# A hybrid decoder layer on one core: GpSimd leaves the attention stage, the compressed branch and the scores are spaced anew, the probabilities' factor is shared by VectorE and ScalarE

## The chip, the cores and the metric

One core of a Trainium2 chip runs the whole layer. The metric is the device time in microseconds (us) of one execution; three executions of the kernel before are known, and one more was recorded by the hardware profiler.

## The reference

One layer, 512 positions, width 1024, float32. A normalised input is projected; three mixers (a gated MLP, "a"; sparse attention, "b"; a recurrent block, "c") each go through a matrix of their own, are weighted by a sigmoid gate and summed; then an output projection and a SwiGLU block follow. The change touches the attention and the sum of branch a:

```python
s_c = where(valid_c, qh @ kc.T * scale, NEG_INF)         # compressed: 31 block keys a head
o_cmp = (softmax(s_c) * any(valid_c)) @ vc
o_slc = softmax(masked(q @ k_slc.T * scale)) @ v_slc     # 8 blocks in 512 positions, all of them chosen
o_win = softmax(masked(q @ k_win.T * scale)) @ v_win     # window 512: also plain causal attention
o = g[..., 0:1] * o_cmp + g[..., 1:2] * o_slc + g[..., 2:3] * o_win
merged = gate_a * (y_a @ w_br_a) + gate_b * (y_b @ w_br_b) + gate_c * (y_c @ w_br_c)
```

There are 16 heads in 4 groups; a group shares keys and values. Top 16 of only 8 blocks chooses all, so the selected and the window branch (br 0 and 1) are both causal attention with their own keys and values.

## The kernel before, in words

**Weights.** Every product runs as three passes over a high and a low part of the operands. A weight tile of 128x1024 is fetched by a DMA of the SP queue into one of two `raw` buffers (`wload`, L168), ScalarE copies it to `hi` (L114), and another engine subtracts to get `lo`: VectorE (L119), or GpSimd (L117) for every third tile of the list `wpool`, that is of the weights used in the attention stage (L158, L193). Three `hi` and three `lo` buffers run ahead of TensorE.

**The attention stage** is `attention(fills)` (L868). For each group `g` there is a list of fill work: gates and products of branch a (`gate_part`, `branch_part`), then the two query tiles, the key tile and, for every second group, the value tiles of the next group. A fill generator yields after every 6 matmuls of 512 columns; each yield is a slot. In each slot `steps(g, 22)` gives out a share of the group's attention, planned so that it lasts 22 slots: `scores(j)` of a unit (a block of 128 queries, one or both branches), `turn` (four transposes of probabilities, L838, and their split into `ph` and `pl`), `values` (two matmuls, L851). A turn comes at least 3 slots after its unit's last score (LAG_T), values 3 slots after their turn (LAG_V); at most three turns run ahead of their values; a unit's scores wait until the unit two before it is turned, because `P` has two buffers. Before the key tile of the next group all scores are given out without fill between them (`while kind == "k"`), because the keys have one buffer. What is left of a group when the fill ends follows without fill.

**The compressed branch** of the next group, `cmp_attn(g + 1)` (L749), has seven steps (scores and mask; maximum, difference, exp; sum and product L773; transposes L777; two value products). Before, its generator begins after both query tiles, one step in every third slot while the group's own steps last, and what is left follows in one go at the group's end.

**A unit's tail** (L826 to L833): after the fourth score, VectorE takes the reciprocals of the sums, multiplies by the gates (L829), and multiplies the probabilities by that factor with one TENSOR_SCALAR for each head and branch, 8 for a unit of both branches (128 or 256 wide), 4 for a unit of one branch (384 or 512 wide).

**The sum of branch a** (`branch_part`, L955): VectorE makes the gated product from PSUM (L966), GpSimd adds it to `merged` (L968). Branch b adds on VectorE (L972).

The issue order on each engine is fixed when the program is built: the framework's scheduler sorts instructions by the order in which they were emitted and by when it estimates them ready, so matmuls of later fills can stand ahead of emitted attention work. On the chip each engine takes its list in order.

Of the kernel before, what the change touches and what calls it, by code (L numbers as in the profile page):

```python
# [25 lines left out]
AF = mybir.ActivationFunctionType  # L26
OP = mybir.AluOpType
# [5 lines left out]
G = 4  # L33
# [17 lines left out]
def hybrid_block(ctx: ExitStack, tc: tile.TileContext, A, out):  # L51
    nc = tc.nc
    V, SC, GP, PE, SY = nc.vector, nc.scalar, nc.gpsimd, nc.tensor, nc.sync
# [33 lines left out]
    def nm(s):  # L87
        cnt[0] += 1
        return f"{s}_{cnt[0]}"
# [8 lines left out]
    def bank(tag):  # L98
        return psum[1].tile([128, S], F32, tag=tag, name=nm(tag), bufs=psum[2][tag])
# [10 lines left out]
    def f32(ap):  # L110
        return ap.bitcast(F32)
# [12 lines left out]
    wlist = []  # L124
# [4 lines left out]
    def w_branch(i, j0=0, j1=8):  # L129
        for j in range(j0, j1):  # L130
            w_in(T_MG + 8 * i + j)
            wlist.append((A["w_br"][i, j], None))
# [11 lines left out]
    w_in(*range(T_U, T_U + 8), *range(T_QKV, T_QKV + 3))  # L144
    wlist += [(A["w_vp"][0, i], None) for i in range(2)]
    FILL = (3, 2, 3, 8)
    w0 = len(wlist)
    fill = []
    for j in range(8):
        fill += [(A["w_in"][T_MG + j], None), (A["w_br"][0, j], None)]  # L150
    for g in range(G):
# [3 lines left out]
            w_in(*range(T_QKV + 3 * g + 3, T_QKV + 3 * g + 6))  # L155
        if g == 1:
            wlist += [(A["w_vp"][1, i], None) for i in range(2)]
    wpool = range(w0, len(wlist))  # L158
    w_branch(1)
    wlist += [(A["w_o"][k], t) for k, t in enumerate(["h"] * 4 + ["f"] + ["m"] * 2 + [None])]  # L160
    HEAD, LAST, LASTV = 3, 4, 2
# [6 lines left out]
    def wload(upto):  # L168
        while wnext[0] < min(upto, len(wlist)):
            i = wnext[0]  # L170
            ap, tag = wlist[i]
            raw = stage.tile([128, 1024], F32, tag="raw", name=nm("raw"), bufs=2)
            parts = [slice(0, 512), slice(512, 1024)] if i == 0 else [slice(0, 1024)]
            for n, p in enumerate(parts):
                SY.dma_start(raw[:, p], ap[:, p])
                if i == 0:
                    x_in(n + 1)
            if tag == "gate":

                hi = lo = wts.tile([128, 1024], F32R, tag="hi", name=nm("hi"), bufs=3)  # L180
                SC.activation(hi, raw, AF.Copy)
                r, h = (t.rearrange("p (k m) -> p k m", m=128)[:, :, 64:] for t in (raw, hi))
                V.tensor_sub(h, r, f32(h))
                wready[i] = (hi, lo)
                wnext[0] += 1
                continue
            if tag:
                u = slab("u", F32R, tag, (2, 1024))
                hi, lo = u[:, 0], u[:, 1]
            else:  # L190
                hi = wts.tile([128, 1024], F32R, tag="hi", name=nm("hi"), bufs=3)
                lo = wts.tile([128, 1024], F32R, tag="lo", name=nm("lo"), bufs=3)
            todo = [(raw[:, p], hi[:, p], lo[:, p], GP if i in wpool and i % 3 == 2 else V) for p in parts]  # L193
            if i == 0:
                wfirst.extend(todo)
            else:
                split(*todo[0])
            wready[i] = (hi, lo)
            wnext[0] += 1
# [33 lines left out]
    def x_in(k):  # L233
        SY.dma_start(xt[k], A["xT"][:, k, :])
# [558 lines left out]
    class Unit:  # L793
# [14 lines left out]
        def scores(self, j):  # L808
            g, a, n, brs = self.g, self.a, self.n, self.brs
            w = len(brs)  # L810
            if j == 0:
                self.T = slab("P", tag="P")
                self.st = mid.tile([128, 3, 4, w], F32, tag="ast", name=nm("ast"), bufs=3)
            st, K = self.st, at[g]["k"]
            ps = bank("sc")
            lhs = at[g]["q"][:, j, a * 128:(a + 1) * 128]
            for i in range(2):
                PE.matmul(ps[:, :w * n].rearrange("p (b n) -> p b n", b=w), lhs, K[:, i, brs[0]:brs[-1] + 1, :n],  # L818
                          start=(i == 0), stop=(i == 1))
            for b, br in enumerate(brs):  # L820
                t = self.part(j, br)
                V.tensor_tensor_reduce(out=t, in0=ps[:, b * n:b * n + n], in1=mask[0][:, S - n:], scale=-0.125,  # L822
                                       scalar=3.0e38, op0=OP.add, op1=OP.min, accum_out=st[:, 0, j, b:b + 1])
                SC.activation(t, t, AF.Exp, scale=-1.0, bias=st[:, 0, j, b:b + 1],  # L824
                              accum_out=st[:, 1, j, b:b + 1])
            if j == 3:  # L826
                V.reciprocal(st[:, 2], st[:, 1])
                for b, br in enumerate(brs):
                    V.tensor_mul(st[:, 2, :, b], st[:, 2, :, b], gates[:, a, 12 * g + 1 + br:12 * g + 12:3])  # L829
                for i in range(4):  # L830
                    for b, br in enumerate(brs):
                        t = self.part(i, br)
                        V.tensor_scalar(t, t, st[:, 2, i, b:b + 1], None, op0=OP.mult)  # L833

        def turn(self, br, kt):
            pt = bank("tr")
# [31 lines left out]
    def attention(fills):  # L868


        slot = [0]
        LAG_T, LAG_V, LAG_C = 3, 3, 3

        def steps(g, slots):

            units = [Unit(g, 0, (0, 1)), Unit(g, 1, (0, 1))] + [Unit(g, a, (br,)) for a in range(2, 4) for br in range(2)]
            SQ = [(n, j) for n in range(len(units)) for j in range(4)]
            TQ = [(n, b) for n, u in enumerate(units) for b in u.blocks]
            VQ = list(TQ)
            sdone, tdone, tslot = {}, {}, {}  # L880
            cs = lambda n: 2 * max(107, 53 * (units[n].a + 1)) / 1e3
            left = sum(cs(n) for n, _ in SQ) + len(TQ) * 0.41 + len(VQ) * 0.43
            k = 0
            while SQ or TQ or VQ:
                room = left / max(slots - k, 1)
                k += 1
                t = slot[0]
                ns = 0
                while room > 0:
                    if VQ and tslot.get(VQ[0], 1e9) + LAG_V <= t:  # L890
                        n, b = VQ.pop(0)
                        units[n].values(*b)
                        c = 0.43
                    elif TQ and sdone.get(TQ[0][0], 1e9) + LAG_T <= t and len(TQ) + 3 > len(VQ):
                        n, b = TQ.pop(0)
                        units[n].turn(*b)
                        tslot[n, b] = t
                        if b == units[n].blocks[-1]:
                            tdone[n] = t
                        c = 0.41  # L900
                    elif SQ and ns < 2 and (SQ[0][0] < 2 or SQ[0][0] - 2 in tdone):
                        n, j = SQ.pop(0)
                        ns += 1
                        units[n].scores(j)
                        if j == 3:
                            sdone[n] = t
                        c = cs(n)
                    else:
                        break
                    room -= c  # L910
                    left -= c
                yield bool(SQ)

        for g, fill in enumerate(fills):
            body = steps(g, 22)
            nxt = cmp_attn(g + 1) if g < G - 1 else iter(())
            wait = 0
            more = True
            have_q = 0
            for kind, gen in fill:  # L920
                while kind == "k" and more:
                    more = next(body, False)
                    slot[0] += 1
                for _ in gen:
                    slot[0] += 1
                    if next(body, None) is None:
                        more = False
                        done.add(g)
                    elif have_q == 2:
                        wait += 1  # L930
                        if wait % LAG_C == 0:
                            next(nxt, None)
                have_q += kind == "q"
            for _ in body:
                slot[0] += 1
            for _ in nxt:
                pass

    def yb_split():
        yb["h"], yb["l"] = Pair("ybh", F32R, "y"), Pair("ybl", F32R, "y")  # L940
# [14 lines left out]
    def branch_part(b, j, y):  # L955

        ps = bank("mm")
        yield from matrix(ps, y["h"], y["l"])
        if "m" not in mg:
            mg["m"] = Pair("merged", tag="m")  # L960
        t = mg.pop((b, j))
        m = mg["m"][j]
        if b == "c":
            V.scalar_tensor_tensor(m, t, 1.0, ps, op0=OP.add, op1=OP.mult)
        else:
            V.scalar_tensor_tensor(t, t, 1.0, ps, op0=OP.add, op1=OP.mult)  # L966
            if b == "a":
                GP.tensor_add(m, m, t)  # L968
            else:
                if j == 0:  # L970
                    mg["h"], mg["l"] = Pair("mh", F32R, "mo"), Pair("ml", F32R, "mo")
                V.tensor_add(m, m, t)  # L972
                split(m, mg["h"][j], mg["l"][j])


# [328 lines left out]
```

## Time and profile before

| | |
|---|---|
| three runs | median 1175.07 us (1173.71 to 1175.76) |
| profiled execution | 1174.67 us, its span 1172.6 us |
| busy in the span | TensorE (PE) 1141.2 us, VectorE (DVE) 695.3, ScalarE (ACT) 512.6, GpSimd (POOL) 91.6 |
| attention stage, 381 to 669 us | 288.0 us: PE 280.13, DVE 255.30, ACT 179.89, POOL 33.61 |

A row of the timeline has start, duration, engine, line, operation and tiles, count, and in brackets the idle time of the engine before it with what ended it. A row with a count above 1 is a run of like instructions, from the first start to the last end. Matmuls are pipelined: one of 512 columns is shown 0.39 us long, and the next starts about 0.23 us after it, so what TensorE lost is read from starts, not from busy time.

### The profile page before, as it was taken

To read this page: it belongs to the slowest core of one execution; us is meant where nothing else is said; L and a number is where in the kernel's file an instruction comes from. 1 tells how busy PE (TensorE), PEld (TensorE's weight loads), DVE (VectorE), ACT (ScalarE), POOL (GpSimd) and SP (SyncE) were. 2 spreads that over 40 slices of the span, in tenths; PEclk is the share of its full clock that TensorE was granted. 3 is DMA by queue.
4 is the path that set the end of the run, shared out by engine and by line. 5 is a ranking of instruction groups with operands and counts; after the bars stand their busy time and mean duration, and the time that the engine had idled before them with its cause. 6 is when DMAs were issued, how large, how long until landed. Compare 5 with 4: busy or idle time off the path is not lost.

```text
span 1172.6 us, 14400 instructions
## 1 busy us (share of the span) xinstructions
PE 1141.2 (97%) x5524; PEld 948.5 (81%) x5524; DVE 695.3 (59%) x1345; ACT 512.6 (44%) x904; POOL 91.6 (8%) x72
## 2 busy tenths in 40 slices
PE   9999699999999999999999999999999999999997
PEld 7878477888889787787877888889988888888885
DVE  5974856554575989988998743458333333332324
ACT  6746456232344667665664532344322322332221
POOL 0000702410000101002011100000000000000001
PEclk9999999999999999999999999999999999999999
DMA  8232222522222211111101162332123233233331
GB/s 310 91 107 72 72 73 91 199 91 90 90 90 73 72 55 37 54 55 54 55 21 54 58 211 93 123 110 89 55 90 106 92 93 105 90 120 96 92 106 72
DMA packets 30373, 108.62 MB, mean 93 GB/s; under 512 B 3649, under 2 KB 3793, under 8 KB 29153
## 3 DMA queue, kind: packets, MB, share of 16 engines
q1 hardware_dynamic: 27792, 98.58, 25.9%
q10 hardware_dynamic: 2448, 9.05, 2.2%
q8 instruction: 43, 0.70, 0.3%
q14 instruction: 26, 0.20, 0.1%
q0 software_dynamic: 64, 0.08, 0.0%
HBM read 105.60 MB, written 2.10 MB: 92 GB/s over the span
## 4 chain that ended last, share of the span: by engine, by line
PE 86%; DVE 8%; ACT 3%; issue 1%; DMA 1%; POOL 1%; DVEq 0%; ACTq 0%; POOLq 0%
PE mm L214 55%; PE mm L1105 10%; PE mm L1005 4%; PE o L851 3%; PE mm L506 3%; PE sc L818 3%; PE tr L838 3%; PE mm L734 2%; DVE P L833 1%; PE tr L650 1%; DVE lo L119 1%; PE tr L432 1%; DVE ti L459 1%; PE tr L756 1%; PE tr L566 1%
## 5 line engine op out<-in xcount | busy, mean ns | idle before, releaser
L114 ACT ACTIVATE hi<-raw 128x1024 fp32r<-128x1024 f32 (+1 forms) x162 | 170.7, 1054 | 371.7 <-PE mm L214 170.0
L119 DVE TENSOR_TENSOR lo<-raw,hi 128x1024 fp32r<-128x1024 f32 (+1 forms) x153 | 188.6, 1233 | 220.3 <-ACT hi L114 213.4
L214 PE MATMUL mm<-hh,hi 128*128 128x512 f32 x504 | 201.2, 399 | 0.0
L214 PE MATMUL mm<-hh,lo 128*128 128x512 f32 x504 | 198.5, 394 | 2.5 <-DVE lo L119 2.5
L214 PE MATMUL mm<-hl,hi 128*128 128x512 f32 x504 | 198.6, 394 | 0.0
L214 PE MATMUL mm<-fh,hi 128*128 128x512 f32 (+1 forms) x336 | 127.6, 380 | 0.0
L214 PE MATMUL mm<-fl,hi 128*128 128x512 f32 (+1 forms) x336 | 127.3, 379 | 0.0
L214 PE MATMUL mm<-fh,lo 128*128 128x512 f32 (+1 forms) x336 | 127.3, 379 | 0.0
L214 PEld LDWEIGHTS mm<-hh,lo 128*128 128x128 f32 x504 | 95.5, 189 | 22.8 <-DVE lo L119 3.3
L214 PEld LDWEIGHTS mm<-hl,hi 128*128 128x128 f32 x504 | 95.4, 189 | 18.9 <-issue 0.2
L214 PEld LDWEIGHTS mm<-hh,hi 128*128 128x128 f32 x504 | 95.5, 189 | 18.4 <-issue 0.2
L1105 PE MATMUL mm<-hi,f 128*128 128x512 f32 x320 | 99.4, 389 | 0.0
L824 ACT ACTIVATE P<-P,ast 128x128 f32<-128x128 f32 (+3 forms) x128 | 70.7, 555 | 30.0 <-DVE ast L822 29.9
L214 PEld LDWEIGHTS mm<-fh,hi 128*128 128x128 f32 x336 | 63.2, 188 | 11.9
L214 PEld LDWEIGHTS mm<-fh,lo 128*128 128x128 f32 x336 | 63.2, 188 | 11.9
L214 PEld LDWEIGHTS mm<-fl,hi 128*128 128x128 f32 x336 | 63.2, 188 | 11.6
L1105 PEld LDWEIGHTS mm<-hi,f 128*128 128x128 f32 x320 | 60.1, 188 | 12.4
L114 ACT ACTIVATE ph<-tr 128x512 fp32r<-128x512 f32 x80 | 46.5, 592 | 48.6 <-PE tr L838 40.4
L1105 PE MATMUL mm<-lo,f 128*128 128x512 f32 x160 | 62.2, 389 | 0.0
L119 DVE TENSOR_TENSOR pl<-tr,ph 128x512 fp32r<-128x512 f32 x80 | 54.2, 686 | 12.5 <-ACT ph L114 11.7
L822 DVE CUSTOM_DVE_ANT_0 P<-sc,mask 128x128 f32<-128x128 f32 (+3 forms) x128 | 58.3, 484 | 4.9 <-PE sc L818 4.2
L1062 DVE TENSOR_TENSOR silu<-silu,mm 128x512 f32<-128x512 f32 x22 | 15.1, 687 | 73.1 <-PE mm L214 73.1
(296 smaller groups left out, 1973.5 us busy)
## 6 DMA issues: line engine op xcount, KB each, us to landing
raw<-in_w_in SPq DMA_DIRECT2D x64, 512.0 KB, 3.5
raw<-in_w_fi SPq DMA_DIRECT2D x44, 512.0 KB, 3.4
raw<-in_w_br SPq DMA_DIRECT2D x24, 512.0 KB, 3.5
raw<-in_w_fo SPq DMA_DIRECT2D x22, 512.0 KB, 3.5
w<-in_cw ACTq DMA_DIRECT2D x4, 1024.0 KB, 5.9
raw<-in_w_o SPq DMA_DIRECT2D x8, 512.0 KB, 3.5
raw<-in_w_v SPq DMA_DIRECT2D x7, 512.0 KB, 5.1
xt<-in_xT SPq DMA_DIRECT2D x8, 256.0 KB, 5.9
```

The costliest lines, as they stand in the source:

```text
L114: SC.activation(hi, src, AF.Copy)
L119: res["lo"] = V.tensor_sub(lo, src, f32(hi))
L214: res["mm"] = PE.matmul(ps[:m, n0:n1], w[:, k * 128:k * 128 + m], x[k][:, n0:n1], start=(t == 0), stop=(t == 3 * NK - 1))
L506: res["mm"] = PE.matmul(b[c], x[k][:, c * 128:(c + 1) * 128], w[:, kk * 512:kk * 512 + 512], start=(k == 0 and t == 0), stop=(k == NK - 1 ...
L734: PE.matmul(ps, x[k][:, q], w[:, ws], start=(k == 0 and t == 0), stop=(k == NK - 1 and t == 2))
L818: PE.matmul(ps[:, :w * n].rearrange("p (b n) -> p b n", b=w), lhs, K[:, i, brs[0]:brs[-1] + 1, :n], start=(i == 0), stop=(i == 1))
L822: V.tensor_tensor_reduce(out=t, in0=ps[:, b * n:b * n + n], in1=mask[0][:, S - n:], scale=-0.125, scalar=3.0e38, op0=OP.add, op1=OP.min, a ...
L824: SC.activation(t, t, AF.Exp, scale=-1.0, bias=st[:, 0, j, b:b + 1], accum_out=st[:, 1, j, b:b + 1])
L838: PE.transpose(pt[:, j * 128:(j + 1) * 128], self.part(j, br)[:, kt * 128:(kt + 1) * 128], ident)
L851: PE.matmul(po, VV[:, kt, g % 2, br].rearrange("p i d -> p (i d)"), x, start=(br == 0 and kt == 0 and t == 0), stop=(br == 1 and kt == a a ...
L1005: res["mm"] = PE.matmul(b[c, f], x[k][:, q], w[:, fs], start=(k == 0 and t == 0), stop=(k == NK - 1 and t == 2))
L1105: PE.matmul(b[c], x[k][:, q], w[:, ws], start=(k == 0 and t == 0), stop=(k == NFF - 1 and t == 2))
```

## The change

1. GpSimd gets no work in the attention stage: the low parts of the `wpool` weights and the sum of branch a go to VectorE.
2. The factor (gate over sum): a unit of both branches has one TENSOR_TENSOR for each branch, over all four heads, with the factor broadcast. A unit of one branch has heads 0 and 1 on ScalarE (a copy with a scale, one instruction for each head) and heads 2 and 3 in one TENSOR_TENSOR on VectorE.
3. A group's steps begin only in the fourth slot of its fill (LAG_K = 3), and are planned over 19 slots.
4. The compressed branch of the next group goes on one step in every fourth slot, over the group's end, through what follows without fill and into the next group's fill. Values of a group wait until its compressed branch has been given out (`cmp_done`).

```diff
-            todo = [(raw[:, p], hi[:, p], lo[:, p], GP if i in wpool and i % 3 == 2 else V) for p in parts]
+            todo = [(raw[:, p], hi[:, p], lo[:, p], V) for p in parts]
...
-                for i in range(4):
-                    for b, br in enumerate(brs):
-                        t = self.part(i, br)
-                        V.tensor_scalar(t, t, st[:, 2, i, b:b + 1], None, op0=OP.mult)
+                own = 0 if w == 2 else 2
+                for i in range(own):
+                    t = self.part(i, brs[0])
+                    SC.activation(t, t, AF.Copy, scale=st[:, 2, i, 0:1])
+                for b, br in enumerate(brs):
+                    o = b * n
+                    t = self.T[:, own:4, o:o + n]
+                    V.tensor_tensor(t, t, st[:, 2, own:4, b:b + 1].to_broadcast([128, 4 - own, n]), op=OP.mult)
...
-        LAG_T, LAG_V, LAG_C = 3, 3, 3
+        LAG_T, LAG_V, LAG_C, LAG_K = 3, 3, 4, 3
...
-                    if VQ and tslot.get(VQ[0], 1e9) + LAG_V <= t:
+                    if VQ and tslot.get(VQ[0], 1e9) + LAG_V <= t and g in cmp_done:
...
+        cmp_done = {0}
+        nxt = [iter(())]
+        wait = [0]
+
+        def cmp_step():
+            wait[0] += 1
+            if wait[0] % LAG_C == 0:
+                next(nxt[0], None)
+
+        def compressed(g):
+            yield from cmp_attn(g)
+            cmp_done.add(g)
+
         for g, fill in enumerate(fills):
-            body = steps(g, 22)
-            nxt = cmp_attn(g + 1) if g < G - 1 else iter(())
-            wait = 0
+            body = steps(g, 22 - LAG_K)
             more = True
             have_q = 0
+            age = 0
             for kind, gen in fill:
                 while kind == "k" and more:
                     more = next(body, False)
                     slot[0] += 1
+                    cmp_step()
                 for _ in gen:
                     slot[0] += 1
-                    if next(body, None) is None:
+                    age += 1
+                    cmp_step()
+
+                    if age > LAG_K and next(body, None) is None:
                         more = False
                         done.add(g)
-                    elif have_q == 2:
-                        wait += 1
-                        if wait % LAG_C == 0:
-                            next(nxt, None)
                 have_q += kind == "q"
+                if have_q == 2:
+                    have_q = 0
+                    nxt[0] = compressed(g + 1)
             for _ in body:
                 slot[0] += 1
-            for _ in nxt:
-                pass
+                cmp_step()
+        for _ in nxt[0]:
+            pass
...
-            if b == "a":
-                GP.tensor_add(m, m, t)
-            else:
+            V.tensor_add(m, m, t)
+            if b == "b":
                 if j == 0:
                     mg["h"], mg["l"] = Pair("mh", F32R, "mo"), Pair("ml", F32R, "mo")
-                V.tensor_add(m, m, t)
                 split(m, mg["h"][j], mg["l"][j])
```

## Rows read from the trace of the kernel before

**Rows 1.** The page's first part: busy time, share of the span and instructions of the engines.

```profile
PE 1141.2 (97%) x5524; PEld 948.5 (81%) x5524; DVE 695.3 (59%) x1345; ACT 512.6 (44%) x904; POOL 91.6 (8%) x72
```

**Rows 2.** Busy time of each engine by stage: stretch, its us, then PE, PEld, DVE, ACT, POOL busy (with instructions), granted clock, DMA share, GB/s. The attention stage and all that follows.

```profile
381.00:669.00 288.00, 280.13 (x1453) 229.18 (x1453) 255.30 (x689) 179.89 (x433) 33.61 (x17) 0.99 0.16 52
669.00:1172.60 503.60, 495.85 (x2337) 416.28 (x2335) 202.17 (x285) 152.14 (x217) 6.42 (x5) 0.99 0.32 102
```

**Rows 3.** Waits of PE between 375 and 672 us: who waited for whom, us in total, times, the longest.

```profile
PE tr L838 <- DVE P L833: 2.6, 2, 1.4
PE sc L818 <- DVE ast L822: 2.4, 2, 2.2
PE tr L777 <- DVE pc L773: 1.8, 1, 1.8
```

**Rows 4.** Timeline of PE around those waits, four places.

```profile
401.46 0.40 PE L214 MATMUL mm<-hl,hi 128*128 128x512 f32 x1
403.08 0.33 PE L838 MATMUL tr<-ident,P 128*128 128x128 f32 x1 [1.22 <-DVE P L833]
...
532.51 0.49 PE L838 MATMUL tr<-ident,P 128*128 128x128 f32 x3
534.43 0.77 PE L838 MATMUL tr<-ident,P 128*128 128x128 f32 x5 [1.43 <-DVE P L833]
...
539.31 0.52 PE L818 MATMUL sc<-K,q 128*128 128x384 f32 x2
...
596.29 0.39 PE L214 MATMUL mm<-yah,hi 128*128 128x512 f32 x1
596.51 0.39 PE L214 MATMUL mm<-yal,hi 128*128 128x512 f32 x1
598.67 0.63 PE L777 MATMUL tr<-ident,pc 128*128 128x128 f32 x4 [1.77 <-DVE pc L773]
...
630.61 0.39 PE L214 MATMUL mm<-hh,lo 128*128 128x512 f32 x1
633.16 0.73 PE L818 MATMUL sc<-K,q 128*128 128x512 f32 x2 [2.16 <-DVE ast L822]
...
635.31 0.77 PE L851 MATMUL o<-ph,V 128*128 128x512 f32 x1 [0.73 <-DVE yb L858]
...
638.30 0.39 PE L214 MATMUL mm<-hl,hi 128*128 128x512 f32 x1
```

**Rows 5.** Timeline of DVE at the same places.

```profile
398.99 4.29 DVE L833 TENSOR_SCALAR P<-P,ast 128x256 f32<-128x256 f32 x8
...
529.76 4.82 DVE L833 TENSOR_SCALAR P<-P,ast 128x128 f32<-128x128 f32 x8
...
595.85 2.67 DVE L773 TENSOR_TENSOR pc<-pc,pcst 128x512 f32<-128x512 f32 x1
...
628.66 3.50 DVE L833 TENSOR_SCALAR P<-P,ast 128x384 f32<-128x384 f32 x4
```

**Rows 6.** Timeline of POOL at the same places.

```profile
400.34 2.53 POOL L117 TENSOR_TENSOR lo<-raw,hi 128x1024 fp32r<-128x1024 f32 x1 [18.38 <-ACT hi L114]
...
529.92 1.29 POOL L968 TENSOR_TENSOR merged<-merged,tg 128x512 f32<-128x512 f32 x1 [23.00 <-DVE tg L966]
531.72 2.38 POOL L117 TENSOR_TENSOR lo<-raw,hi 128x1024 fp32r<-128x1024 f32 x1 [0.51 <-ACT hi L114]
...
595.60 2.38 POOL L117 TENSOR_TENSOR lo<-raw,hi 128x1024 fp32r<-128x1024 f32 x1 [30.82 <-ACT hi L114]
...
628.57 2.40 POOL L117 TENSOR_TENSOR lo<-raw,hi 128x1024 fp32r<-128x1024 f32 x1
```

**Rows 7.** Timeline of DVE elsewhere in the stage: the same instructions with POOL idle.

```profile
461.30 1.65 DVE L833 TENSOR_SCALAR P<-P,ast 128x128 f32<-128x128 f32 x8
...
469.57 2.18 DVE L833 TENSOR_SCALAR P<-P,ast 128x256 f32<-128x256 f32 x8
...
495.25 1.67 DVE L833 TENSOR_SCALAR P<-P,ast 128x512 f32<-128x512 f32 x4
...
515.11 0.69 DVE L773 TENSOR_TENSOR pc<-pc,pcst 128x512 f32<-128x512 f32 x1
...
546.10 1.39 DVE L833 TENSOR_SCALAR P<-P,ast 128x384 f32<-128x384 f32 x4
```

**Rows 8.** Groups of instructions by line and shape, 381 to 669 us (the one of L972: 400 to 760 us): count, then busy us, mean ns of one, then idle time before them.

```profile
L117 POOL TENSOR_TENSOR lo<-raw,hi 128x1024 fp32r<-128x1024 f32 x9 | 21.9, 2436 | 245.9 <-ACT hi L114 245.9
L968 POOL TENSOR_TENSOR merged<-merged,tg 128x512 f32<-128x512 f32 x8 | 14.4, 1798 | 133.6 <-DVE tg L966 121.5 <-DVE ast L827 12.1
...
L119 DVE TENSOR_TENSOR lo<-raw,hi 128x1024 fp32r<-128x1024 f32 x19 | 23.2, 1219 | 2.4 <-ACT hi L114 2.3
...
L972 DVE TENSOR_TENSOR merged<-merged,tg 128x512 f32<-128x512 f32 x8 | 5.5, 691 | 0.2
...
L768 ACT ACTIVATE pc<-pc 128x512 f32<-128x512 f32 x4 | 2.5, 628 | 1.1 <-DVE pc L766 1.0
```

**Rows 9.** The attention stage cut near the beginnings of the four groups; columns as in rows 2.

```profile
381.00:448.00 67.00, 65.61 (x337) 53.56 (x336) 59.77 (x169) 43.22 (x106) 7.18 (x4) 1.00 0.20 64
448.00:521.00 73.00, 72.90 (x421) 61.04 (x420) 68.10 (x189) 47.96 (x115) 7.31 (x3) 1.00 0.12 37
521.00:589.00 68.00, 66.30 (x330) 53.87 (x329) 59.88 (x163) 42.96 (x105) 8.26 (x4) 0.97 0.19 63
589.00:669.00 80.00, 75.33 (x371) 60.72 (x369) 67.55 (x171) 45.74 (x109) 10.86 (x6) 0.98 0.15 47
```

More of the change, by code (lines that the diff above doesn't have):

```diff
@@ L146, in hybrid_block @@
     FILL = (3, 2, 3, 8)
-    w0 = len(wlist)
     fill = []
@@ L157, in hybrid_block @@
             wlist += [(A["w_vp"][1, i], None) for i in range(2)]
-    wpool = range(w0, len(wlist))
     w_branch(1)
```

## The prediction

> **What bounds the kernel now.** I read the page's first part before anything else: PE is busy 97% of the span, VectorE 59% [rows 1]. PE is the engine whose list sets the end, and the change takes no matmul away, so all that can be won is time in which PE stands still or runs slowly. Then the stages: behind the attention stage PE is busy 495.85 of 503.60 us, and nothing there is changed [rows 2]. In the attention stage it is 280.13 of 288.00, and there VectorE is at 255.30 of 288.00, 89%, where the span's mean hides it [rows 2]. So the question is whether VectorE makes PE wait, and the view of PE's waits says that it does: the longest all end with VectorE, and there are few of them, five in three lines [rows 3].
>
> The timeline of PE has them at four places [rows 4]. A matmul's shown end lies past the next one's start (596.29 and 596.51 in rows 4: 0.22 to 0.23 us from start to start), so the loss is read from starts:
> - 401.46 to 403.08, less the 0.23 of one matmul: 1.4 us.
> - 532.51 to 539.31, 6.8 us, in which PE did 8 transposes (0.11 each, from three in 0.49), 4 score matmuls of 384 columns (0.17) and 6 fill matmuls (0.23): 3.0 us of work, 3.8 lost. [...]
> - 596.51 to 598.67, less 0.23: 1.9 us.
> - 630.61 to 638.30, 7.7 us, in which PE started the work of 13 matmuls of 512 columns (3.0 us): 4.7 lost, again partly at the lower level (granted 0.98) [rows 9].
>
> Together 11.8 us.
>
> Now what VectorE did there. Eight multiplications of 128 columns took 4.82 us, eight of 256 took 4.29, four of 384 took 3.50, and one product of the compressed branch 2.67 [rows 5]. Elsewhere the same instructions take 1.65, 2.18, 1.39 and 0.69 [rows 7]. At each of the four places GpSimd is in an instruction of 1.29 to 2.53 us, and the excess (3.17, 2.11, 2.11, 1.98, together 9.4 us) is about what is left of GpSimd's instruction when VectorE's next one comes [rows 5 to 7]. So VectorE, reading and writing SBUF alone, is held until GpSimd is through, and PE behind it. An order laid down when the program was built could not allow for that.
>
> **The change part by part.**
>
> *No work on GpSimd.* Removed: 9 subtractions and 8 additions, 36.3 us of POOL [rows 8], and with them the 9.4 us of hold. Added to VectorE: 9 at 1.22 and 8 at 0.69, 11.0 + 5.5 = 16.5 us [rows 8]. The raw buffer of a weight comes free after a subtraction of 1.22 us in VectorE's line and not after 2.44 on POOL, so SP's transfers start neither much earlier nor later; at 52 GB/s [rows 2] they are no bound. On VectorE the subtraction now stands ahead of turns and scores: up to 1.22 us of delay for them, at a place the scheduler knows.
>
> *The factor.* A group now has 8 of 128, 8 of 256, 8 of 384 and 8 of 512 columns: 1.65 + 2.18 + 2 x 1.39 + 2 x 1.67 = 9.95 us, 39.8 for four groups [rows 7]. After: two products of 4 x 128, priced as L773, 0.69 each [rows 7]; two of 4 x 256, priced as the subtraction over 1024, 1.22 [rows 8]; two of 2 x 384, between these two, 0.95; two of 2 x 512, 1.22. That is 8.2 a group, 32.6 in all: 7.2 us less on VectorE. ScalarE gets 32 copies; the nearest row is its 512-wide exponential of the compressed branch, 0.63 [rows 8], so at most 20 us onto 179.90 [rows 2]: 200, and it stays 80 us under PE. The copy waits on ScalarE for VectorE's reciprocal and product, and behind it in ScalarE's line stand the evictions of turns and the next exponentials. No row has such a wait; a bound is 0 (scheduled into a gap) to about 1.2 us (one long VectorE instruction in front) for 16 units. I take nothing from it for PE, as turns have three slots of lag, and keep 2 us in the range.
>
> [...] The rows decide for the saving at the narrow end (eight of 128 in 1.65 us against two of 512 in 1.38 [rows 7]), since there the instruction count weighs, and leave about even at 256.
>
> *VectorE's sum:* -9.4 - 7.2 + 16.5 = -0.1 us. The load stays at 255 us, but none of it is a surprise any more. If PE loses nothing, the stage lasts 288.0 - 11.8 = 276.2 us, and VectorE is at 92%. The second stretch shows that this is enough: from 448 to 521 us VectorE is at 68.10 of 73.00, 93%, and PE at 72.90 [rows 9].
>
> *Scores four parts behind their keys.* For three slots a group's fill runs alone: 3 x 6 x 0.23 = 4.1 us with no new scores for VectorE. What lies in that time is the last group's turns and sums, the four subtractions of the new keys, and now the compressed branch. If that cover is gone, VectorE loses 4.1 us a group. The end is closer too: the last group has 24 slots, its steps now start in the fourth, so a little more of its turns and values falls behind the fill. What hides that is the first gate product of branch b, 24 matmuls of 0.23 or 5.5 us, which needs nothing of attention and which the scheduler may pull up. Cost 0 to 3 us; I take 1.
>
> *The compressed branch spaced.* Its VectorE work is unchanged, and issues no DMA. Before, most of its steps fall in one go at a group's end; now one in four slots. The new wait: values of a group are not given out until all seven steps are. Following the loop slot by slot, the first values stood in a group's 8th slot before; after the change they stand in the 11th of groups 0 and 2, which is the lag alone, and in the 12th of groups 1 and 3, one slot of holding. As only three turns may run ahead, the held values hold turns, and those the scores of the third and fourth unit: that work is then squeezed into fewer slots. Cost: 0 (the scheduler pulls later fill up) to 4 x 1.4 = 5.5 us for each of the two groups; I take 1 each.
>
> *Sum.* 1174.67 (the profiled execution, span 1172.6 and 2.1 around it) - 11.8 + 1 + 2 = 1165.9. The median of the runs lies 0.4 above the profiled one: 1166.
>
> **The rivals.**
>
> *A, VectorE is the bound.* Its busy time doesn't fall, and its 32.7 idle us in the stage [rows 2] are waits for scores and for ScalarE that don't go away with GpSimd; then the waits of PE come back elsewhere, most of the 11.8 is spent again, and the time is 1171 to 1176, middle 1173.5. [...] For it: 89% busy, and a sum that is zero. Against it: the 93% stretch without a wait [rows 9].
>
> *B, slower.* The place is the beginning of a group. If VectorE is short of work in the three lag slots and the held values, and short of time behind them, each group gets longer by the lag: 4 x 4.1 = 16.4 us, so 1174.7 - 11.8 + 16.4 = 1179.3. It decides from the point at which PE has no fill left to pull up while scores are given out, that is when the fills' three product banks are full. For it: in the second group a larger part of the scores now falls ahead of the key tile without fill (7 slots by the loop, before 4). Against it: key and value tiles follow directly, 17 us of matmuls, and VectorE is as busy with the tails and the compressed branch at these boundaries as anywhere.
>
> *C, the spacing does nothing,* because the scheduler re-sorts it, and only GpSimd's part counts; also, subtraction and addition take GpSimd's very places, 1.91 us for 3.73. Then about half of the 11.8 stays: 1169. That lies in the forecast's range.
>
> **How the numbers follow.** Forecast with C (1160.5 to 1171): 0.68. Its lower end is all of 11.8 and 2 us of smaller waits. A (1171 to 1176): 0.17. B (around 1179): 0.15. About 0.2% is what a measurement of this kernel can tell from no change, here 2.3 us; faster by more is below 1172.7: 0.68 and 0.07 of A, 0.75. Within it: 0.10 of A. Slower: B, 0.15. The range reaches from 1160.5 to the end of A, 1176, and leaves out B and a little.
>
> **What would show it.** No POOL instruction in the stage; VectorE's factor at about 8 us a group and no SBUF instruction of it two to four times its usual length; PE's waits for `P` and `pc` gone, granted clock 1.00 in all four stretches; the stage 278 to 282 us long. It is wrong if the stage has as many waits of PE on VectorE as before, elsewhere (A), if PE stands at the beginnings of groups or in front of values (B), or if ScalarE's scaled copies hold the evictions of turns.

## Result and the profile after

The changed kernel takes 1165.11 us, median of 6 runs (1163.15 to 1168.17), against 1175.17 of the kernel before (6 runs, 1172.76 to 1175.76): a ratio of 0.9919, 95% interval 0.9902 to 0.9936. It is faster by 10.1 us; the prediction said 1166.

The profiled run of after took 1168.17, the highest of the six, with a span of 1166.4. The three parts of the span beside those of before: up to the first score matmul of the compressed branch 383.6 us, before 379.7; the attention stage, from that matmul to the start of its last value matmul, 278.9 us, before 289.1; what follows, 503.9 and 503.8 us. The 4.0 us ahead of the stage belong to this one run: there the granted clock between 200 and 250 us was 0.93, and a second profile of the same kernel (e10, below) comes to the stage at 378.1 us. So the gain is the stage's, 10.2 us of it, and the rest of the text goes by the stage. Two profiles of one kernel agree on it within 0.2 us (after and e10 both 278.9; e4 and e11, below, 278.4 and 278.3).

The page's first part, after; it answers to [rows 1]:

```profile
PE 1140.9 (98%) x5524; PEld 949.6 (81%) x5524; DVE 690.6 (59%) x1266; ACT 532.8 (46%) x936; POOL 55.2 (5%) x55
```

PE did the same 5524 matmuls in 0.3 us less; what went, over the whole span of this run, is time in which it stood still. Within the stage its busy time fell too, as the next rows show, but ahead of the stage this run had the lower clock just told. GpSimd has 17 instructions and 36.4 us less, VectorE 79 instructions less and 4.7 us less although it took over those 17, ScalarE 32 more, the scaled copies.

The stages, after; columns as in [rows 2]. The first four lines answer to [rows 9], with the same cuts, and the last is the stage from its first to its last matmul:

```profile
381.00:448.00 67.00, 66.98 (x361) 55.96 (x360) 58.64 (x147) 49.00 (x114) 0.00 (x0) 1.00 0.17 56
448.00:521.00 73.00, 72.98 (x426) 61.76 (x425) 68.52 (x164) 53.85 (x124) 0.00 (x0) 1.00 0.13 44
521.00:589.00 68.00, 67.73 (x348) 55.51 (x347) 60.93 (x152) 49.37 (x117) 0.00 (x0) 1.00 0.17 55
589.00:669.00 80.00, 78.29 (x387) 63.46 (x386) 68.46 (x159) 52.02 (x119) 0.00 (x0) 1.00 0.22 71
...
383.60:662.90 279.30, 277.30 (x1467) 229.06 (x1466) 253.52 (x613) 201.58 (x466) 0.00 (x0) 1.00 0.16 54
```

The same line of before:

```profile
379.60:669.10 289.50, 281.63 (x1467) 230.66 (x1467) 255.82 (x691) 181.14 (x434) 35.11 (x17) 0.99 0.16 52
```

Read the last line against it: the same 1467 matmuls in 10.2 us less. PE's idle time fell from 7.9 to 2.0 us, and its busy time by 4.3 us, most of which is time at a lower granted clock: it is 1.00 in all four stretches, where it was 0.97 and 0.98 in the last two [rows 9]. In before it was low at two places, the second and the fourth of [rows 4]; columns as in [rows 2]:

```profile
535.00:540.00 5.00, 4.79 (x16) 3.66 (x15) 3.89 (x19) 3.70 (x12) 0.00 (x0) 0.66 0.31 105
...
630.00:635.00 5.00, 2.42 (x10) 1.36 (x8) 4.89 (x11) 0.82 (x2) 0.97 (x1) 0.97 0.34 105
635.00:640.00 5.00, 4.69 (x19) 3.92 (x20) 2.35 (x8) 2.54 (x7) 0.00 (x0) 0.69 0.00 0
```

At the first of them PE's timeline has matmuls of 512 columns that start 0.43 us apart, where those at 596.29 and 596.51 us [rows 4] are 0.22 apart:

```profile
537.30 0.63 PE L214 MATMUL mm<-hl,hi 128*128 128x512 f32 x1
537.73 0.63 PE L214 MATMUL mm<-hh,lo 128*128 128x512 f32 x1
538.16 0.63 PE L214 MATMUL mm<-hh,hi 128*128 128x512 f32 x1
```

An estimate from the granted clocks: what is missing to 1.00 is 0.34 of 5 us at the first place, 0.03 and 0.31 of 5 us at the second, so PE lost some 1.7 us at each. VectorE's busy time fell by 2.3 us only, so its share went up, from 88 to 91%, while PE's long waits for it went away.

PE's waits between 375 and 672 us, after; they answer to [rows 3]:

```profile
PE o L854 <- DVE pl L119: 1.1, 1, 1.1
PE o L854 <- DVE yb L861: 0.4, 2, 0.2
PE tr L841 <- DVE pl L119: 0.3, 1, 0.3
PE o L854 <- ACT ph L114: 0.2, 1, 0.2
```

The waits for `P` and `pc`, and those of the scores for `ast`, are gone. What is left is 2.0 us, and the longest of it is new: a value matmul for the low half of a turn. It stands at the very end of the stage, as PE's timeline shows:

```profile
660.94 0.49 PE L854 MATMUL o<-ph,V 128*128 128x512 f32 x1
...
662.52 0.50 PE L854 MATMUL o<-pl,V 128*128 128x512 f32 x1 [1.09 <-DVE pl L119]
662.86 0.39 PE L212 MATMUL mm<-hh,hi 128*128 128x512 f32 x1
```

and VectorE's timeline shows what it was doing while PE waited for that `pl`:

```profile
658.85 1.28 DVE L119 TENSOR_TENSOR pl<-tr,ph 128x512 fp32r<-128x512 f32 x2
660.05 0.68 DVE L119 TENSOR_TENSOR ybl<-yb,ybh 128x512 fp32r<-128x512 f32 x1
660.65 1.22 DVE L119 TENSOR_TENSOR lo<-raw,hi 128x1024 fp32r<-128x1024 f32 x1
661.78 0.69 DVE L119 TENSOR_TENSOR pl<-tr,ph 128x512 fp32r<-128x512 f32 x1
```

A split of branch b's input and one of a weight, 1.9 us together, stand in line ahead of the last turn.

The groups of VectorE's instructions by line and shape, 381 to 669 us, after: a weight's subtraction, which the nine of GpSimd have joined, and the factor's products (count, then busy us, mean ns of one, idle time before them):

```profile
L119 DVE TENSOR_TENSOR lo<-raw,hi 128x1024 fp32r<-128x1024 f32 x29 | 35.3, 1218 | 5.1 <-ACT hi L114 4.1 <-PE o L854 0.7
...
L836 DVE TENSOR_TENSOR P<-P,ast 128x1024 f32<-128x1024 f32 x16 | 19.2, 1220 | 0.2
...
L836 DVE TENSOR_TENSOR P<-P,ast 128x768 f32<-128x768 f32 x8 | 7.6, 953 | 0.1
...
L836 DVE TENSOR_TENSOR P<-P,ast 128x512 f32<-128x512 f32 x8 | 5.2, 686 | 0.0
```

The factor on VectorE is 19.2 + 7.6 + 5.2, 32.0 us in all. And on ScalarE, the scaled copies, in the same view:

```profile
L832 ACT ACTIVATE P<-P,ast 128x512 f32<-128x512 f32 x16 | 10.7, 714 | 1.5 <-DVE ast L827 1.5
L832 ACT ACTIVATE P<-P,ast 128x384 f32<-128x384 f32 x16 | 8.9, 608 | 3.1 <-DVE ast L827 3.1
```

19.6 us, and 4.6 us of waiting for VectorE's reciprocal and gates; none of PE's waits above ends with a scaled copy.

### The profile page after: what moved, and what is told of

Same layout as the page of the kernel before. It is cut to its first block, busy times and chain, and to the rows that moved or that the text cites. A ratio compares the mean times of both kernels' runs of the same rounds, so it can differ in the third digit from the quotient of the medians.

```text
span 1166.4 us, 14306 instructions
## 1 busy us (share of the span) xinstructions
PE 1140.9 (98%) x5524; PEld 949.6 (81%) x5524; DVE 690.6 (59%) x1266; ACT 532.8 (46%) x936; POOL 55.2 (5%) x55
## 4 chain that ended last, share of the span: by engine, by line
PE 87%; DVE 7%; DMA 3%; ACT 2%; issue 1%; POOL 1%; SPq 0%; DVEq 0%; ACTq 0%; POOLq 0%
PE mm L212 57%; PE mm L1122 10%; PE mm L1022 4%; PE sc L816 3%; PE o L854 3%; PE tr L841 3%; PE mm L732 2%; DVE lo L119 1%; PE tr L648 1%; PE tr L430 1%; DMA wabr<-in_wab 1%; DMA xrow<-in_x 1%; DVE ti L457 1%; PE tr L564 1%; DMA xt<-in_xT 1%
## 5 line engine op out<-in xcount | busy, mean ns | idle before, releaser
L119 DVE TENSOR_TENSOR lo<-raw,hi 128x1024 fp32r<-128x1024 f32 (+1 forms) x162 | 199.6, 1233 | 220.4 <-ACT hi L114 212.6
L212 PEld LDWEIGHTS mm<-hh,lo 128*128 128x128 f32 x504 | 95.7, 190 | 22.8 <-DVE lo L119 3.4
L212 PEld LDWEIGHTS mm<-fh,hi 128*128 128x128 f32 x336 | 63.2, 188 | 11.8
```

The source lines that it names most:

```text
L119: res["lo"] = V.tensor_sub(lo, src, f32(hi))
L212: res["mm"] = PE.matmul(ps[:m, n0:n1], w[:, k * 128:k * 128 + m], x[k][:, n0:n1], start=(t == 0), stop=(t == 3 * NK - 1))
```

## The experiments

The theory was the prediction's, called **H** (hold): a VectorE instruction that only touches SBUF and comes up while GpSimd is in one stands until that one is through, and PE behind it; a gain comes from GpSimd's work being gone, wherever it ran. Two rivals for the same gain. **L** (lateness): what PE waited for were GpSimd's own results, which take 2.44 us for VectorE's 1.22 [rows 8], so the work counts and not the meeting. **S** (order): the spacing of edits 3 and 4 took the crowd away from the groups' ends, and GpSimd's part is small. Below, edit 1 is no work on GpSimd, edit 2 the factor shared with ScalarE, edit 3 the scores' lag and edit 4 the compressed branch's spacing. Ratios are to the kernel before on the same chip, 5 rounds each, with their 95% intervals.

**e1_gpsimd_off.** Before, with edit 1 alone:

```diff
-            todo = [(raw[:, p], hi[:, p], lo[:, p], GP if i in wpool and i % 3 == 2 else V) for p in parts]
+            todo = [(raw[:, p], hi[:, p], lo[:, p], V) for p in parts]
...
-                GP.tensor_add(m, m, t)
+                V.tensor_add(m, m, t)
```

> The kernel before with edit 1 alone: the low parts of the weights and the sum of branch a go from GpSimd to VectorE; factor, lag and spacing stay as before. Theory H (GpSimd's instructions hold VectorE's SBUF instructions, and TensorE waits behind these): nearly the whole gain, 1164 to 1169 us, the waits at the four places gone. Rival S (the gain comes from the new order of scores and compressed branch): VectorE gets 16.5 us of work and the order is the old one, so 1172 to 1177. Rival F (VectorE is the bound and the shared factor makes room): 1170 to 1175.

Measured: 1163.97 against 1173.72, 0.9911 (0.9894 to 0.9929). The stage lasts 278.4 us, no longer than that of the whole change. The stage in e1, first to last matmul, columns as above:

```profile
380.10:658.90 278.80, 276.91 (x1467) 228.95 (x1466) 257.47 (x707) 181.01 (x434) 0.00 (x0) 1.00 0.16 54
```

VectorE has 1.7 us more to do than before and is at 92%, and PE loses 1.9 us where it had lost 7.9. So edit 1 brings the whole gain. S isn't needed for it, and rival A of the prediction falls: a VectorE at 92% doesn't bound this stage. L is not excluded by it, though in the kernel before none of PE's waits in the stage ends with GpSimd [rows 3].

**e2_gpsimd_back.** After, with edit 1 undone (the diff of e1 turned round).

> The kernel after with edit 1 undone: the same 9 subtractions and 8 additions on GpSimd again. Theory H: the holds come back at whatever VectorE instructions now meet GpSimd, 1171 to 1177 us, with several products by the factor at two to four times their usual length. Rival S: the order is the new one, and VectorE is relieved of 16.5 us, so 1162 to 1167.

Measured: 1168.84, 0.9957 (0.9940 to 0.9974); the stage lasts 283.4 us, 4.5 more than after. That is below what H expected and above what S did: not quite half of the gain goes. VectorE was held 5 times for 4.2 us, against 9 times for 12.3 us in before. "Held" here and below is counted from the records: a VectorE instruction that runs beside one of GpSimd (of those that begin in the stage) and takes over 0.12 us more than the lower quartile of its own line and shape; the excess over that quartile is the time held.

**e3_gpsimd_unneeded.** After, with GpSimd work of the same number and size that nobody waits for, behind VectorE's own; the output is unchanged. The list `wpool` is put back for it, and the main lines are:

```diff
...
                 split(*todo[0])
+                if i in wpool and i % 3 == 2:
+                    GP.tensor_sub(raw, raw, f32(hi))
...
             V.tensor_add(m, m, t)
+            if b == "a":
+                GP.tensor_add(t, t, t)
```

> The kernel after, with GpSimd work added that no engine waits for: after VectorE's subtraction, GpSimd writes raw minus hi into the raw buffer of the same 9 weights (only the next transfer into that buffer waits for it), and after VectorE's addition it doubles the gated product in place, 8 times, when nothing reads it any more. VectorE keeps all its work. Theory H: the holds alone cost, so several us come back, 1168 to 1177, and TensorE's waits end with VectorE instructions that overlap a GpSimd one. [...]

Measured: 1167.55, 0.9943 (0.9927 to 0.9960); the stage lasts 282.5 us, 3.6 more than after, though no result of GpSimd is needed. The time is just under H's 1168 and well over that of after, which L, with no result awaited, would keep; so the time alone doesn't decide; the trace does. GpSimd's timeline in e3, one line:

```profile
499.11 2.39 POOL L199 TENSOR_TENSOR raw<-raw,hi 128x1024 f32<-128x1024 f32 x1 [29.93 <-DVE ast L831]
```

VectorE's at that time:

```profile
499.56 3.01 DVE L840 TENSOR_TENSOR P<-P,ast 128x1024 f32<-128x1024 f32 x1
```

and PE's:

```profile
501.02 0.27 PE L845 MATMUL tr<-ident,P 128*128 128x128 f32 x1
502.63 0.44 PE L845 MATMUL tr<-ident,P 128*128 128x128 f32 x2 [1.34 <-DVE P L840]
```

GpSimd is in its unneeded subtraction until 501.50. VectorE's product, 1.22 us in after, begins at 499.56 and takes 3.01: 501.50 and one undisturbed product more is 502.72, its end is 502.57. The turn waits 1.34 us for it. No result of GpSimd is in that chain, so this hold is H and not L. It accounts for 1.3 of the 3.6 us. The next largest wait that after doesn't have, 1.0 us at 472.25 us, comes behind a product of the gates on VectorE that was held for 1.4 us at 467.68; the remaining 1.2 us are not traced.

**e9_gpsimd_twice.** Before, with each of GpSimd's subtractions done twice (the second writes the same values again):

```diff
             GP.tensor_sub(lo, src, f32(hi))
+            GP.tensor_sub(lo, src, f32(hi))
```

> The kernel before with each of GpSimd's 9 subtractions done twice, the second writing the same again: 22 us more of POOL in the stage. Theory H: more of VectorE's SBUF instructions meet it; in the runs so far TensorE's loss in the stage is 11.1 us and 0.7 to 0.9 of the held time of VectorE (12.3 us held in the kernel before), so with about 18 to 22 us held the time is 3 to 9 us over the kernel before, 1177 to 1183 where that is 1174. Rival (what costs is only how late the nine low parts are): each is 2.4 us later, TensorE has them three tiles ahead, so 0 to 1 us.

Measured: 1184.97 against 1174.82, 1.0087 (1.0072 to 1.0102), more than H's 1177 to 1183 and far from the 0 to 1 us of lateness; none of PE's waits in the stage ends with GpSimd here either. The stage lasts 301.2 us, and VectorE is held 13 times for 21.3 us. The worst place, VectorE's timeline in e9:

```profile
636.65 5.59 DVE L834 TENSOR_SCALAR P<-P,ast 128x384 f32<-128x384 f32 x4
```

and GpSimd's:

```profile
636.56 2.40 POOL L117 TENSOR_TENSOR lo<-raw,hi 128x1024 fp32r<-128x1024 f32 x1
639.04 2.34 POOL L118 TENSOR_TENSOR lo<-raw,hi 128x1024 fp32r<-128x1024 f32 x1
```

Four multiplications that take 1.39 us undisturbed [rows 7] take 5.59: they are held by one instruction of GpSimd and then by the next. The first two of PE's waits in e9, of the whole stage:

```profile
PE sc L819 <- DVE ast L823: 5.8, 3, 4.2
PE tr L839 <- DVE P L834: 4.3, 3, 1.6
```

The lines are those of [rows 3], longer.

Stage and time held of all kernels with GpSimd work, each beside the kernel that differs from it only in that GpSimd has none (in all but e3 VectorE then does that work); GpSimd's time is that of the instructions that begin in the stage (e6 and e7 to e11 are told below):

| kernel | GpSimd busy in stage, us | VectorE held: times, us | stage, us | the one without | over it |
|---|---|---|---|---|---|
| e9 | 54.1 | 13, 21.3 | 301.2 | e1, 278.4 | 22.8 |
| before | 34.0 | 9, 12.3 | 289.1 | e1, 278.4 | 10.7 |
| e6 | 34.1 | 7, 8.1 | 285.3 | e4, 278.4 | 6.9 |
| e2 | 30.0 | 5, 4.2 | 283.4 | after, 278.9 | 4.5 |
| e3 | 32.2 | 5, 4.2 | 282.5 | after, 278.9 | 3.6 |
| e7 | 31.8 | 4, 4.8 | 283.5 | e8, 281.6 | 1.9 |

The stage goes by the time held, about one for one in five of the six, and not by how much GpSimd does: 30 to 34 us of GpSimd work cost from 1.9 to 10.7 us. In e7 more than half of the time held cost nothing.

**e6_factor_alone.** Before, with edit 2 alone, as in the diff of the change.

> The kernel before with edit 2 alone: the factor as one broadcast product for each branch, or half of it on ScalarE; GpSimd keeps its work, the old order stays. Theory H: fewer of VectorE's instructions can be held (48 instead of 128 for the factor), but the same GpSimd work meets them, so part of the gain: 1166 to 1173 us. Rival F (VectorE's own time, 7 us less, is what counts): 1164 to 1168. If the replaced instructions only move the meeting points: 1172 to 1177.

Measured: 1170.38 against 1174.05, 0.9968 (0.9956 to 0.9980), in H's range and above F's. The factor takes 32 of VectorE's instructions, not the 48 of the expectation. The stage is 285.3 us; VectorE is held 7 times, 8.1 us. The first of PE's waits in e6:

```profile
PE o L856 <- DVE yb L863: 3.8, 3, 3.3
```

The longest of the three is 3.3 us, where before had 0.7 for the same line [rows 4]. PE's timeline has it here:

```profile
627.19 0.77 PE L856 MATMUL o<-ph,V 128*128 128x512 f32 x1 [3.33 <-DVE yb L863]
```

The sum of the values, `yb`, ends this wait but is not itself held; ahead of it VectorE's timeline has the factor:

```profile
621.53 3.12 DVE L838 TENSOR_TENSOR P<-P,ast 128x768 f32<-128x768 f32 x1
624.58 1.29 DVE L863 TENSOR_TENSOR yb<-yb,o 64x256 f32<-64x256 f32 x3
```

and GpSimd's one subtraction:

```profile
621.42 2.42 POOL L117 TENSOR_TENSOR lo<-raw,hi 128x1024 fp32r<-128x1024 f32 x1
```

The product, 0.95 us undisturbed, took 3.12. It is the fourth meeting of before (GpSimd's instruction at 628.57 us [rows 6], VectorE's at 628.66 [rows 5]) once more: the shorter factor did not move it.

**e7_spacing_alone.** Before, with edits 3 and 4 alone, as in the diff.

> The kernel before with edits 3 and 4 alone: scores behind their keys, compressed branch spaced, values held; GpSimd keeps its work, the old factor stays. Theory H: the meeting points of GpSimd and VectorE move, their number doesn't, and the last group's end costs about 2 us: 1171 to 1178 us. Rival S: 1165 to 1170.

Measured: 1168.80, 0.9958 (0.9946 to 0.9971): H had expected 1171 to 1178, and that is missed; the time is where S put it. The stage is 283.5 us with GpSimd at 31.8 us, little less than in before, but VectorE is held only 4 times, 4.8 us. Without GpSimd the same spacing doesn't shorten the stage: with the old factor it goes from 278.4 (e1) to 281.6 us (e8, below), with the new one from 278.4 (e4, next) to 278.9. So S is right that the spacing by itself would have brought about half of the gain, but the counts say that it does so by fewer and other meetings, and beside edit 1 nothing is left for it. The parts don't add: 10.7 us for edit 1 alone, 5.6 for e7, 3.8 for e6, and 10.2 for all. Whether the spaced order has fewer meetings by rule or by luck stays open.

**e4_no_spacing and e11_no_spacing_same_chip.** After with edits 3 and 4 undone, that is before with edits 1 and 2; e11 is the same kernel once more, beside e10, on one chip.

> The kernel after with edits 3 and 4 undone (old order of scores, compressed branch and values), edits 1 and 2 kept. Theory H: the order is worth little, 1162 to 1168 us. Rival S: 1171 to 1176, with waits of TensorE for VectorE at the beginnings of groups.

> Edits 1 and 2 without 3 and 4, as in the earlier run, on the same chip as the kernel after. Theory T: 0.990 of the kernel before, 1.5 to 2.5 us under the kernel after. If the spacing is worth something without GpSimd: at or above the kernel after.

Measured: e4 1162.32, 0.9899 (0.9880 to 0.9918); e11 1162.01 against 1174.82, 0.9892 (0.9877 to 0.9907). The stage is 278.4 and 278.3 us. That is H's range, and S's 1171 to 1176 is out.

**e10_after_same_chip.** After once more.

> The kernel after, unchanged, on the same chip as the next one. Theory T (the spacing, edits 3 and 4, costs about 2 us at the last group's end): 0.992 of the kernel before.

Measured: 1163.14 against the same 1174.82, 0.9906 (0.9890 to 0.9922), stage 278.9 us. The intervals of e10 and e11 overlap: the spacing costs about 1 us or nothing, less than the 1.5 to 2.5 that T expected. Where it wins and loses is in the windows. The last 15 us of the stage and what lies ahead of them, in after:

```profile
383.60:648.00 264.40, 264.09 (x1402) 219.15 (x1401) 239.95 (x592) 192.07 (x451) 0.00 (x0) 1.00 0.17 55
648.00:663.00 15.00, 13.31 (x67) 10.01 (x66) 13.57 (x22) 9.51 (x16) 0.00 (x0) 1.00 0.11 37
```

and in e4:

```profile
378.50:642.40 263.90, 262.87 (x1392) 216.96 (x1391) 239.22 (x593) 191.63 (x452) 0.00 (x0) 1.00 0.15 53
642.40:657.40 15.00, 15.00 (x77) 12.46 (x76) 10.92 (x19) 8.15 (x14) 0.00 (x0) 1.00 0.19 70
```

e4 does 77 matmuls in its last 15 us, 0.195 us each, after 67. So after is ahead by 10 matmuls when the last 15 us begin, an estimated 2.0 us at that rate, having used 0.5 us more: it has won 1.5. Then it loses 2.0. VectorE is busy 13.57 of these 15 us, against 10.92. e10 and e11 show the same at this cut, 1403 against 1392 matmuls ahead of it.

**e5_tail_order.** After, with the splits of branch b's input queued on VectorE behind the split of the last turn, so that they no longer stand ahead of it:

```diff
-        for k in range(NK):
-            split(yb["y"][k], yb["h"][k], yb["l"][k])
+        with tc.issue_after(res["lo"].ins):
+            for k in range(NK):
+                split(yb["y"][k], yb["h"][k], yb["l"][k])
```

> The kernel after, with one line of order: VectorE's eight subtractions that split the attention's result are queued behind the subtraction of the last turn, which they stand ahead of in the kernel after (there TensorE waits some 3 us in all near 660 us, mostly for that turn). Theory T (the spacing costs its 2 us at the last group's end, where the last turns queue on VectorE behind these splits): the loss near 660 us goes from 3.1 to about 1 us, the time 1.5 to 2.5 us under the kernel after, that is at the 0.990 of the kernel without spacing. Rival G (the loss at the end comes from the late values and their lag, not from the order on VectorE): no change, 0.992.

Measured: 1162.70 against 1174.05, 0.9907 (0.9893 to 0.9920); stage 278.1, 0.8 us less than after. That is neither T's 1.5 to 2.5 us nor G's nothing, and the time alone can't be told from that of e10 (0.9906). PE's waits in e5:

```profile
PE tr L841 <- DVE pl L119: 0.7, 1, 0.7
PE o L854 <- DVE yb L861: 0.5, 2, 0.3
PE o L854 <- DVE pl L119: 0.2, 1, 0.2
```

The long wait of after is 0.2 us here, but a turn now waits 0.7 for the `pl` before it. That the splits stood in the way is part of the loss at the end, the smaller part: e5 does 70 matmuls in its last 15 us, after 67, e4 77. That the rest comes from the last units being late there is argued, not shown.

**e8_factor_old.** After, with edit 2 undone.

> The kernel after with edit 2 undone: no GpSimd, new order, but the factor in 128 products on VectorE, nothing of it on ScalarE. VectorE has 7 us more. Theory H: with nothing to hold VectorE, it still fits under TensorE: 0 to 2 us more than the kernel after (0.992 to 0.994). Rival F: 3 to 7 us more, with waits of TensorE for VectorE through the stage.

Measured: 1166.67, 0.9939 (0.9926 to 0.9951), stage 281.6 us. The stage in e8:

```profile
377.80:659.80 282.00, 278.93 (x1468) 228.55 (x1467) 259.78 (x709) 182.74 (x434) 0.00 (x0) 1.00 0.15 53
```

VectorE is 6.3 us busier than in after, and the stage 2.7 us longer, between H's 0 to 2 and F's 3 to 7. PE's idle time is 3.1 us against 2.0, so the waits account for 1.1 of the 2.7; where the rest is lost the rows don't tell. In the order of before the same edit brings nothing to the stage (e1 and e4 both 278.4 us; the times, 0.9911 against 0.9899 and 0.9892, have intervals that overlap). So the factor pays only beside the spacing. That the spaced order needs the room on VectorE that edit 2 makes is a likely reason, not shown, and which of the two, lag or held values, would need it was not tried.

The lowest ratios are those of e4 and e11, edits 1 and 2 without the spacing, 0.990 and 0.989; but e1, e4, e5, e10 and e11 lie within 0.2% of one another, with intervals that overlap.

## Why the prediction was right

**The hold.** Predicted: 11.8 us of PE's time at four places, from 9.4 us in which GpSimd held VectorE. Measured: 10.7, the stage of before against that of e1 (289.1 - 278.4). e3 shows the mechanism with a GpSimd that nobody waits for, e9 the dose. The count over the whole stage finds 9 holds with 12.3 us, the four places of [rows 4] being the long ones. The term was 1.1 us too large: it took all of PE's loss at the four places as won, and e1 has small waits of its own, 1.9 us. The prediction's wording, VectorE "reading and writing SBUF alone", is a little too wide, as the last section shows.

**VectorE's sum.** Predicted -0.1 us; measured 255.82 to 253.52, -2.3. The three terms: the nine subtractions and eight additions came at the prices taken, 1.218 and 0.683 us for 1.219 and 0.691 [rows 8]; the factor at 32.0 for the 32.6 predicted, 0.953 us for the 768 columns that had no row; and the holds were 12.3, not 9.4. One of the nine, 1.1 us, falls to a split at 669.02 us, behind all but 0.1 us of the window of 255.82, so 11.2 of them count here: -11.2 - 7.8 + 16.5 = -2.5, for -2.3 measured.

**The factor.** It fell from 39.8 [rows 7] to 32.0 us on VectorE, 7.8 less, where 7.2 were predicted. A product of two tensors takes 0.686 us for 512 elements and 1.220 for 1024, 1.04 ns for each one more. A multiplication of 128 columns takes 0.21 us and one of 512, four times as wide, 0.42 (eight in 1.65, four in 1.67) [rows 7]. From these two an estimate of the part of an instruction's time that doesn't depend on its width is 0.14 us, and there were 128 such instructions, now 32 on VectorE. ScalarE's part, bound at 20 us, was 19.6, and no wait of PE ends with it.

**The closer end and the spacing.** Predicted +1 and +2; measured +2.0 in the last 15 us and -1.5 ahead of them. The sum, +3 predicted, is +0.5. The closer end was under-priced: the prediction had the first gate product of branch b cover it, but PE's list has that product only behind the last value matmul (its first matmul starts at 662.86 us), and VectorE's splits for branch b and a weight's stand ahead of the last turn; the splits for branch b are worth 0.8 us by e5. The held values were over-priced: ahead of the end nothing was lost, the zero end of the bound. What brought the 1.5 us there is open, since edits 3 and 4 were never run apart.

**The rivals.** A fell with e1, VectorE at 92% and PE's loss down from 7.9 to 1.9 us. B had its place wrong: in after PE stands at the end of the last group and not at the beginnings. C expected that subtraction and addition in GpSimd's places keep half of the loss; 1.22 us at a place known to the scheduler cost nothing that the stage shows. C's other half, that the spacing does nothing, holds to within 1 us beside edits 1 and 2. So the predicted 1165.9 rests on two errors of opposite sign, a hold 1.1 us too large and new waits 2.5 us too large, and hits the median of 1165.11 by 0.8. That it comes so close is partly luck; that GpSimd's hold was the cause, and its size to 10%, is not.

Not settled: why the factor helps only the spaced order, what the spacing wins ahead of the stage's end, and whether the fewer meetings of e6 and e7 come by rule.

## What to carry to other kernels

Look at a GpSimd instruction by what VectorE does beside it: VectorE instructions that took two to four times their usual length with GpSimd busy at that moment (4.29 us for 2.18 in before [rows 5, 7], 5.59 for 1.39 in e9) were holds, and with VectorE at 89% of the stage, as in before, the time held was lost about one for one in five of the six kernels with GpSimd work in it. Then moving the work onto an engine that is 89% busy can be right, as it was here, where its instructions are shorter on that engine (1.22 us for 2.44 [rows 8]). Price a change at the place where its cover ends, the last group, apart from the rest, and undo each part by itself: here one of four brought the whole gain.

## What the runs showed that was not expected

VectorE's instructions that read PSUM were not held. GpSimd's timeline in e2, one subtraction:

```profile
425.73 2.40 POOL L117 TENSOR_TENSOR lo<-raw,hi 128x1024 fp32r<-128x1024 f32 x1 [24.41 <-ACT hi L114]
```

and VectorE's beside it:

```profile
425.91 0.69 DVE L822 CUSTOM_DVE_ANT_0 P<-sc,mask 128x512 f32<-128x512 f32 x1
426.53 0.08 DVE L822 DVE_READ_ACCUMULATOR2_ANT ast<- 128x1 f32 x1
426.53 0.69 DVE L822 CUSTOM_DVE_ANT_0 P<-sc,mask 128x512 f32<-128x512 f32 x1
```

Two score instructions, with one input from PSUM, run at their usual 0.69 us (0.686 in after) inside GpSimd's 2.40. Not all that stays in SBUF is held, either. In the kernel before GpSimd's timeline has an addition:

```profile
404.91 1.28 POOL L968 TENSOR_TENSOR merged<-merged,tg 128x512 f32<-128x512 f32 x1 [2.04 <-DVE tg L966]
```

and VectorE's beside it a reciprocal of sums in SBUF, at its usual length, and behind it a product of sums and gates that is held for 0.3 us:

```profile
405.36 0.16 DVE L827 RECIPROCAL ast<-ast 128x4 f32<-128x4 f32 x1
405.44 0.38 DVE L858 TENSOR_TENSOR yb<-yb,o 64x256 f32<-64x256 f32 x1
405.75 0.47 DVE L829 TENSOR_TENSOR ast<-ast,gates 128x4 f32<-128x4 f32 x1
```

Over the stages of all kernels, of VectorE's instructions that began with more than 0.3 us of a GpSimd one still to go, all 40 products and differences with nothing but SBUF inputs were held, none with an input from PSUM, and none of 13 reciprocals. What a piece of GpSimd work costs is therefore decided by which VectorE instruction comes next, and that is how some 30 us of it can cost 2 or 11. Even a product of 4 columns is held: in e9 one of the gates' products took 1.26 us beside GpSimd's addition of 1.29, where it takes 0.16 alone.
